# Paired down projection, gate activation and kept sums rearranged in a hybrid encoder layer

## The chip, the core and the metric

The kernel runs on one NeuronCore of one Trainium2 chip. The metric is the device time of one launch in microseconds (us). A core has several engines, each with its own queue of instructions that it works through strictly in order: TensorE (PE in the profile, with its weight loads as PEld), VectorE (DVE), ScalarE (ACT), GpSimd (POOL) and SyncE (SP). DMAs are issued from queues of SP, ACT and POOL and then move data beside the engines. Engines wait for one another on semaphores.

## The reference

One layer of an encoder is applied to two groups of tokens, 256 (prompt) and 512 (sample), all in float32, with a model width of 1024. Three token mixers run first (a diagonal state-space model, differential attention and cross-attention into memory); their outputs are merged and added to x. The change touches only what comes last, the feed-forward part with a hidden width of 2816:

```python
    h2 = rmsnorm(x, ffn_norm_g[li])
    g, up = jnp.split(h2 @ w_gate_up[li], 2, axis=-1)
    x = x + (jax.nn.silu(g) * up) @ w_down[li]
```

## The kernel before, in words

**Products.** All 768 tokens are held as one matrix. Each float32 operand is split into a high and a low part in a TensorE format (`fp32r`), and a product is three matmuls that accumulate in one bank of PSUM: high by high, high by low and low by high (`mm3`, L800 to L802). The high part is written by ScalarE as a copy, the low part by VectorE as a difference (`split_evac`, or L592 and L593 for streamed weights). PSUM is shared out as five banks (`psd`) and three (`psb`).

**Feed-forward in hidden blocks.** The hidden width is cut into 11 blocks of 256, numbered 0 to 10. Block 0 is computed plainly. For blocks 1 to 10, gate and up are each one call of `block`, which works out a product of 2x2 block matrices with Strassen-Winograd's seven products instead of eight: left factors A11, A12, S2, S1, S3, S4, A22 (weights, of which the S are sums made by GpSimd, tiles `ws`), right factors B11, B21, T2, T1, T3, B22, T4 (the normed tokens and their sums, made once). VectorE adds the products into tiles `fs` (L1458), and `fin_gate` and `fin_up` turn finished quarters into the hidden activations `fa`. `fin_gate` makes silu as a Tanh on ScalarE (L1413) and one operation on VectorE (L1414), which leaves twice the silu; the factor 0.5 is put right where the activations are split.

**Down projection.** Block 0 goes through `down_first`. Blocks (1,2), (3,4), (5,6) and (7,8) are taken in pairs by `down_pair`, again with seven products; blocks 9 and 10 go plainly through `down_last`. In a pair the left factors are activations (A11 to A22, sums S1 to S4; function `left` splits them on ScalarE at L1496 and VectorE at L1497, `left_sum` adds on VectorE at L1504) and the right factors are weights of `w_down` (T1 to T4 are sums). Each of the seven products takes three PSUM tiles `dn` of 128x512. `into` adds a product to the residual `x1` on VectorE (L1521). Products 1, 6 and 5 (A11·B11, S2·T2, S1·T1), which several quarters of the result need, are kept instead: `keep` copies each third on ScalarE to a tile `de`, stores it by a DMA of ScalarE's queue to `p_scr`, and for pairs after the first adds it to `p_sum` in DRAM by a DMA of GpSimd's queue (L1558). `down_sums` loads these sums once near the end by SP's DMAs and adds them to `x1` in 21 additions (L1598).

**Weights.** A stream (`W`, class `WStream`) loads weight pieces ahead of their use: raw tiles `wr` (three buffers), split tiles `wh`, `wl` (a ring of four), GpSimd's sums `ws`, and for the down projection two tiles `wt..x` and `wt..z` of 512 KB. `_split_d` makes the right factors in the order of their use. It builds T3 = B22 - B12, T2 = T3 + B11 and T4 = B21 - T2 in place in `wt..x`: a negation on ScalarE (L601), then a DMA on GpSimd's queue that adds a part of `w_down` from DRAM (L600). In the names, wh86 is stream piece 86; with pair 4 (blocks 7 and 8) pieces 85 and 86 are its down weights, 87 is gate 9, 88 up 9 and 89 gate 10.

**What sets the order.** The program is written in one order, and the Tile scheduler places the instructions in each engine's queue by its own simulated times and by when buffers come free. On an engine an instruction that waits holds up everything behind it. Three rings matter here: `lf` holds three left halves (high and low); `ft` has three tiles, which Tanh's results, the `de` of `keep` and the `de` of `down_sums` share; `brr` holds `fs` and the left sums `ls`.

Of the kernel before, what the change touches and what calls it, by code (L numbers as in the profile page):

```python
# [504 lines left out]
class WStream:  # L505
# [90 lines left out]
    def _split_d(self, i, h, kind):  # L596

        r = self.raw.pop(2 * i + h)
        (b11, b12), (b21, b22) = (self.src[j][0] for j in ((i, i + 1) if kind == "d" else (i - 1, i)))
        add = lambda t, b: self.nc.gpsimd.dma_start(t.rearrange("p (k c) -> p k c", k=2), b, accum_op=ALU.add)  # L600
        minus = lambda t, x: self.nc.scalar.activation(t, x, AF.Copy, scale=-1.0)  # L601
        new = lambda k: self.wsums.tile([128, self.HALF], F32, name=f"wt{i}{k}", tag="wt")
        if kind == "d" and h == 0:
            self._right(i, "B11", r)
            self.z = new("z")
            minus(self.z, r)
            add(self.z, b12)
        elif kind == "d":
            self.x = new("x")
            minus(self.x, r)  # L610
            add(self.x, b22)
            self._right(i, "T3", self.x)
        elif h == 0:
            add(self.x, b11)
            self._right(i, "T2", self.x)
            self._right(i, "B21", r)
            self._right(i, "T1", self.z)
        else:
            minus(self.x, self.x)
            add(self.x, b21)  # L620
            self._right(i, "T4", self.x)
            self._right(i, "B22", r)

    def _split(self):
        i, h = divmod(self.n_split, 2)
# [44 lines left out]
def hybrid_block(ctx, tc, A, outs, consts):  # L670
# [737 lines left out]
    act_in = {}  # L1408

    def fin_gate(fb, c, m, cs):  # L1410
        n = cs.stop - cs.start
        t = ft_.tile([128, 512], F32, name=uid("ft"), tag="ft")
        act.activation(t[:, 0:n], c, AF.Tanh, scale=0.5)  # L1413
        v.scalar_tensor_tensor(out=act_in[fb][:, m, cs], in0=t[:, 0:n], scalar=1.0, in1=c, op0=add, op1=mul)  # L1414

    def fin_up(fb, c, m, cs):
        o = act_in[fb][:, m, cs]
        v.tensor_tensor(out=o, in0=o, in1=c, op=mul)
        if fb == 0:
            hh, hl = hid[0]  # L1420
            act.activation(hh[:, m, cs], o, AF.Copy, scale=0.5)
            v.scalar_tensor_tensor(out=hl[:, m, cs], in0=o, scalar=0.5, in1=hh[:, m, cs].bitcast(F32),
                                   op0=mul, op1=sub)

    def new_block(what, fb):
        if what == "gate":
# [66 lines left out]
    def left(key, src):  # L1493

        hi, lo = (lf.tile([128, 2, HT], F32R, name=uid(f"l{key}{w}"), tag="l" + w) for w in "hl")
        act.activation(hi, src, AF.Copy, scale=0.5)  # L1496
        v.scalar_tensor_tensor(out=lo, in0=src, scalar=0.5, in1=hi.bitcast(F32), op0=mul, op1=sub)  # L1497
        L[key] = hi, lo
        return hi, lo

    def left_sum(o, x, y, op):
        if o is None:
            o = stg.tile([128, 2, HT], F32, name=uid("ls"), tag="brr")
        v.tensor_tensor(out=o, in0=x, in1=y, op=op)  # L1504
        return o

    def down_begin(fb):

        a = act_in[fb]
        left("A11", a[:, :, 0:HT])  # L1510
        if fb < NFB - 2:
            left("S3", left_sum(None, a[:, :, 0:HT], a[:, :, HT:TOK], sub))

    def out_block(r, c, t):

# [19 lines left out]
    def down_pair(fb):  # L1535

        a, b = act_in.pop(fb), act_in.pop(fb + 1)
        a11, a21, a12, a22 = a[:, :, 0:HT], a[:, :, HT:TOK], b[:, :, 0:HT], b[:, :, HT:TOK]  # L1540
        R = dict(W.get())
        R.update(W.get())

        def prod(l, r):
            ps = banks()
            rh, rl = R.pop(r)
            rows_times(ps, L.pop(l), (lambda k: rh[:, k], lambda k: rl[:, k]), True, True)
            return ps
# [24 lines left out]
        into(0, 1, prod("S4", "B22"))  # L1573

    def down_last(fb):

        a, b = act_in.pop(fb), act_in.pop(fb + 1)
        w = [W.get(), W.get()]
        for r in range(2):
            h = slice(HT * r, HT * r + HT)  # L1580
            x = [L.pop("A11") if r == 0 else left("A21", a[:, :, h]), left("A2", b[:, :, h])]
            ps = [banks(), banks()]
            for i in range(2):
                for c in range(2):
                    y = [(lambda k, j=j: w[i](k, 512 * c, 512)[j]) for j in range(2)]
                    rows_times(ps[c], x[i], y, i == 0, i == 1)
            for c in range(2):
                into(r, c, ps[c], done=True)

    def down_sums():  # L1590

        for t in range(3):
            e = {}
            for key in "165":
                e[key] = ft_.tile([128, 512], F32, name=uid("de"), tag="ft")
                nc.sync.dma_start(e[key], p_sum[key][:, t])
            b = {(r, c): out_block(r, c, t) for r in range(2) for c in range(2)}
            plus = lambda o, y: v.tensor_tensor(out=o, in0=o, in1=y, op=add)  # L1598
            plus(b[0, 0], e["1"])
            plus(e["6"], e["1"])  # L1600
            plus(b[1, 1], e["6"])
            plus(b[1, 0], b[1, 1])
            plus(b[1, 1], e["5"])
            plus(e["6"], e["5"])
            plus(b[0, 1], e["6"])


    with ExitStack() as c5:
# [210 lines left out]
    W.wsums = c6.enter_context(tc.tile_pool(name="wsum2", bufs=2))  # L1819
    for fb in range(1, NFB):  # L1820
        block("gate", fb)
        if fb == NFB - 2:
            down_sums()
        if fb == 2:
            for t in range(3):
                o = out_block(1, 0, t)

                tc.keep_in_program_order(v.tensor_tensor(out=o, in0=o, in1=out_block(1, 1, t), op=sub))
        if fb % 2 == 0:
            down_begin(fb - 1)  # L1830
        block("up", fb)
        if fb % 2 == 0:
            (down_last if fb == NFB - 1 else down_pair)(fb - 1)
# [45 lines left out]
```

## Time and profile before

| | us |
|---|---|
| median of 3 runs | 1785.59 |
| lowest and highest run | 1784.18, 1787.11 |
| profiled execution, its own time | 1780.15 |
| its span | 1778.4 |
| PE busy | 1748.8 (98% of the span) |
| DVE busy | 1307.2 (74%) |
| ACT busy | 917.3 (52%) |
| POOL busy | 252.0 (14%) |

The four paired down projections begin at 1379.52, 1468.75, 1555.80 and 1644.98 us of the span. Behind the fourth stand gate 9 (from 1678.72), up 9 (1693.31) and gate 10 (1707.87). The profile comes from one execution of the program. Its page lists busy times and the costliest groups of instructions; the trace behind it can be asked for every instruction in a stretch of time, with what it waited for. In a timeline row stand the start, the duration, the engine, the line, the operation, what it writes and reads, and in brackets how long its engine stood idle before it and whose end released it. In a row on windows each engine's busy time is followed by its number of instructions.

### The profile page before, as it was taken

The page shows a single profiled execution, that of the slowest core. Times are in us where ns is not written, and L with a number is a line of the kernel's source. Part 1 is how long each engine was busy: PE and PEld are TensorE (multiplying, and loading weights), DVE is VectorE, ACT ScalarE, POOL GpSimd, SP SyncE. Part 2 cuts the span into 40 slices and gives each one's busy share as a digit, 9 for nine tenths or more (in the row PEclk, how much of TensorE's full clock was granted, in tenths as well). Part 3 has the DMA queues.
Part 4 walks back from the last instruction along what each step waited for, and adds up shares of the span by engine and source line. Part 5 has one row for each costly group of instructions (what it writes and reads, how often), then busy time and mean ns, then how long its engine had stood idle before and what let it go on. Part 6 is the DMA issues. An engine that isn't in the chain of part 4 may idle for free. (4 is left out here: it accounts for less than half of the span.)

```text
span 1778.4 us, 29549 instructions
## 1 busy us (share of the span) xinstructions
PE 1748.8 (98%) x11214; PEld 1611.2 (91%) x11214; DVE 1307.2 (74%) x2409; ACT 917.3 (52%) x1894; POOL 252.0 (14%) x283
## 2 busy tenths in 40 slices
PE   8999999999999999999999999999999999999999
PEld 8999988999999998999978888888889898989787
DVE  7655758799999688878885545452689787879795
ACT  7444544777676457778666333232434545454431
POOL 0000000000000101011110101000113333333330
PEclk9999999999999999999999999999999999999999
DMA  7222656655656477554862635322314447474742
GB/s 255 72 96 95 108 136 159 157 138 138 156 136 162 124 173 194 113 114 90 184 166 75 217 117 171 116 97 70 83 44 112 136 114 174 121 179 115 171 130 83
DMA packets 211565, 235.14 MB, mean 132 GB/s; under 512 B 59232, under 2 KB 169056, under 8 KB 211424
## 3 DMA queue, kind: packets, MB, share of 16 engines
q1 hardware_dynamic: 178000, 149.63, 28.1%
q0 software_dynamic: 27088, 71.05, 19.6%
q10 hardware_dynamic: 6336, 12.59, 1.9%
q8 instruction: 88, 1.44, 0.3%
q14 instruction: 53, 0.43, 0.1%
HBM read 163.94 MB, written 49.09 MB: 120 GB/s over the span
## 5 line engine op out<-in xcount | busy, mean ns | idle before, releaser
L638 ACT ACTIVATE wh<-wr 128x1024 fp32r<-128x1024 f32 x130 | 146.8, 1130 | 74.4 <-PE br L801 27.5
L644 DVE TENSOR_TENSOR wl<-wr,wh 128x1024 fp32r<-128x1024 f32 x84 | 111.0, 1322 | 75.4 <-ACT wh L638 74.8
L800 PE MATMUL gl<-Hhi,wh 128*128 128x256 f32 (+1 forms) x384 | 132.2, 344 | 1.0 <-ACT glt L1110 1.0
L802 PE MATMUL gl<-Hhi,wl 128*128 128x256 f32 (+1 forms) x384 | 128.9, 336 | 0.0
L801 PE MATMUL gl<-Hlo,wh 128*128 128x256 f32 (+1 forms) x384 | 128.8, 336 | 0.0
L642 POOL DMA_DIRECT2D wl<-wr x46 | 40.2, 874 | 516.9 <-ACT wl L641 448.5
L800 PE MATMUL qk<-wh,Hhi 128*128 128x256 f32 x384 | 107.5, 280 | 1.1 <-ACT qksq L1176 1.1
L801 PE MATMUL qk<-wl,Hhi 128*128 128x256 f32 x384 | 107.7, 280 | 0.0
L802 PE MATMUL qk<-wh,Hlo 128*128 128x256 f32 x384 | 107.6, 280 | 0.0
L800 PEld LDWEIGHTS gl<-Hhi,wh 128*128 128x128 f32 x384 | 72.2, 188 | 8.3 <-ACT glt L1110 1.2
L802 PEld LDWEIGHTS gl<-Hhi,wl 128*128 128x128 f32 x384 | 72.0, 188 | 8.0
L801 PEld LDWEIGHTS gl<-Hlo,wh 128*128 128x128 f32 x384 | 72.3, 188 | 7.2
L1276 DVE TENSOR_REDUCE nm<-sc 128x1 f32<-128x512 f32 (+1 forms) x96 | 57.2, 599 | 24.4 <-PE sc L1271 23.1
L800 PEld LDWEIGHTS qk<-wh,Hhi 128*128 128x128 f32 x384 | 72.3, 188 | 2.1 <-ACT qksq L1176 1.3
L802 PEld LDWEIGHTS qk<-wh,Hlo 128*128 128x128 f32 x384 | 72.4, 189 | 0.7
L801 PEld LDWEIGHTS qk<-wl,Hhi 128*128 128x128 f32 x384 | 72.3, 188 | 0.5
L563 ACT ACTIVATE wh_S<-ws 128x512 fp32r<-128x512 f32 x70 | 41.3, 624 | 57.6 <-POOL ws L585 36.1
L564 DVE TENSOR_TENSOR wl_S<-ws,wh_S 128x512 fp32r<-128x512 f32 x70 | 56.2, 823 | 15.6 <-ACT wh_S L563 15.4
L1278 ACT ACTIVATE p<-sc,nm 128x512 f32<-128x512 f32 (+1 forms) x96 | 59.1, 617 | 13.3 <-DVE nm L1276 12.8
L1628 ACT ACTIVATE glr<-glr 128x768 f32<-128x768 f32 x24 | 20.3, 846 | 66.0 <-DMA glr<-gl_scr 64.1
L800 PE MATMUL v<-wh,Hhi 128*128 128x256 f32 x192 | 53.9, 281 | 0.0
L801 PE MATMUL v<-wl,Hhi 128*128 128x256 f32 x192 | 53.8, 280 | 0.0
(582 smaller groups left out, 6209.5 us busy)
## 6 DMA issues: line engine op xcount, KB each, us to landing
wr<-in_w_in_dram SPq DMA_DIRECT2D x48, 512.0 KB, 5.0
wl<-wr POOLq DMA_DIRECT2D x46, 512.0 KB, 5.0
wr<-in_w_gate_up_dram SPq DMA_DIRECT2D x44, 512.0 KB, 4.5
wr<-in_w_branch_dram SPq DMA_DIRECT2D x24, 512.0 KB, 4.4
wr<-in_w_down_dram SPq DMA_DIRECT2D x22, 512.0 KB, 4.4
glr<-gl_scr POOLq DMA_DIRECT2D x24, 384.0 KB, 3.6
wr<-in_w_mem_kv_dram SPq DMA_DIRECT2D x16, 512.0 KB, 3.7
wr<-in_w_in_dram SPq DMA_DIRECT2D x32, 256.0 KB, 4.5
```

The source lines that it names most:

```text
L563: self.nc.scalar.activation(f(hi), src, AF.Copy)
L564: self.nc.vector.tensor_tensor(out=f(lo), in0=src, in1=f(hi).bitcast(F32), op=ALU.subtract)
L638: self.nc.scalar.activation(hi, r, AF.Copy)
L642: self.nc.gpsimd.dma_start(lo, r.bitcast(F32R), accum_op=ALU.add)
L644: self.sub.tensor_tensor(out=lo, in0=r, in1=hi.bitcast(F32), op=ALU.subtract)
L800: pe.matmul(ps, wh, xh, start=start, stop=False)
L801: pe.matmul(ps, wh, xl, start=False, stop=False)
L802: pe.matmul(ps, wl, xh, start=False, stop=stop)
L1276: v.tensor_reduce(out=nm[:, m : m + 1], in_=ps, axis=AX.X, op=ALU.max, negate=True)
L1278: act.activation(pm[:, 0:n], ps, AF.Exp, bias=nm[:, m : m + 1], accum_out=s1s[:, tt : tt + 1] if m == 0 else s2)
L1628: act.activation(g, g, AF.Tanh, scale=0.5)
```

## The change

The program is the same up to the first gate block. From there on:

- **Order of the seven products of a pair.** Before: A11·B11, S3·T3, S2·T2, A12·B21, S1·T1, A22·T4, S4·B22. After: A11·B11, S3·T3, A12·B21, S4·B22, S2·T2, S1·T1, A22·T4. The left halves are made in that order too, and `_split_d` makes the right factors as B21, B22, T2, T1, T4, where they were T2, B21, T1, T4, B22.
- **S4.** It was written over S2's sum late in the pair. It is now made early, in a buffer of its own (tag `do`).
- **Gate activation.** ScalarE's Silu writes `fa` in one call per quarter; Tanh, its temporary tile and VectorE's L1414 are gone. The activations are no longer doubled, so the splits need no 0.5 and are a plain copy and a plain subtraction.
- **Kept sums.** `down_sums` takes a tile number. Tile 0 is added behind gate 9's code, tile 1 behind gate 10's, and tile 2 in `down_last`, where all three stood behind gate 9's code.

```diff
@@ _split_d
         elif h == 0:
             add(self.x, b11)
+            self._right(i, "B21", r)
+        else:
+            self._right(i, "B22", r)
             self._right(i, "T2", self.x)
-            self._right(i, "B21", r)
             self._right(i, "T1", self.z)
-        else:
             minus(self.x, self.x)
             add(self.x, b21)
             self._right(i, "T4", self.x)
-            self._right(i, "B22", r)
@@ fin_gate, fin_up
-        n = cs.stop - cs.start
-        t = ft_.tile([128, 512], F32, name=uid("ft"), tag="ft")
-        act.activation(t[:, 0:n], c, AF.Tanh, scale=0.5)
-        v.scalar_tensor_tensor(out=act_in[fb][:, m, cs], in0=t[:, 0:n], scalar=1.0, in1=c, op0=add, op1=mul)
+        act.activation(act_in[fb][:, m, cs], c, AF.Silu)
...
-            act.activation(hh[:, m, cs], o, AF.Copy, scale=0.5)
-            v.scalar_tensor_tensor(out=hl[:, m, cs], in0=o, scalar=0.5, in1=hh[:, m, cs].bitcast(F32),
-                                   op0=mul, op1=sub)
+            split_evac(hh[:, m, cs], hl[:, m, cs], o)
@@ left, left_sum
-        act.activation(hi, src, AF.Copy, scale=0.5)
-        v.scalar_tensor_tensor(out=lo, in0=src, scalar=0.5, in1=hi.bitcast(F32), op0=mul, op1=sub)
+        split_evac(hi, lo, src)
...
-    def left_sum(o, x, y, op):
-        if o is None:
-            o = stg.tile([128, 2, HT], F32, name=uid("ls"), tag="brr")
+    def left_sum(x, y, op, tag="brr", bufs=2):
+        o = stg.tile([128, 2, HT], F32, name=uid("ls"), tag=tag, bufs=bufs)
@@ down_pair
         keep("1", prod("A11", "B11"))
-        s1 = left_sum(None, a21, a22, add)
-        s2 = left_sum(None, s1, a11, sub)
+        left("A12", a12)
+        s1 = left_sum(a21, a22, add)
+        s2 = left_sum(s1, a11, sub)
+        left("S4", left_sum(a12, s2, sub, "do", 1))
+        into(1, 1, prod("S3", "T3"))
         left("S2", s2)
-        into(1, 1, prod("S3", "T3"))
-        left("A12", a12)
+        into(0, 0, prod("A12", "B21"))
+        left("S1", s1)
+        into(0, 1, prod("S4", "B22"))
+        left("A22", a22)
         keep("6", prod("S2", "T2"))
-        left("S1", s1)
-        into(0, 0, prod("A12", "B21"))
-        left("A22", a22)
         keep("5", prod("S1", "T1"))
-        left("S4", left_sum(s2, a12, s2, sub))
         into(1, 0, prod("A22", "T4"))
-        into(0, 1, prod("S4", "B22"))
@@ down_last, down_sums, the loop over blocks
+            if r == 0:
+                down_sums(2)
...
-    def down_sums():
-
-        for t in range(3):
...
+    def down_sums(t):
...
-        if fb == NFB - 2:
-            down_sums()
+        if fb >= NFB - 2:
+            down_sums(fb - NFB + 2)
```

VectorE's queue at the start of pair 4, before: T2's lower part (`wl86_T2`) stands ahead of the two sums `ls` that make S1 and S2.

```order
L593 TENSOR_TENSOR wl86_T2_18100<-wt85x_17999,wh86_T2_18099 128x1024
L1504 TENSOR_TENSOR ls_1943_18208<-fa_1885_17549,fa_1908_17834 128x768
L1458 TENSOR_TENSOR fs_1928_18009<-fs_1928_18009,up_1935_18125 128x384
L593 TENSOR_TENSOR wl86_B21_18104<-wr86_0_17865,wh86_B21_18103 128x1024
L1418 TENSOR_TENSOR fa_1908_17834<-fa_1908_17834,fs_1928_18009 128x384
L1504 TENSOR_TENSOR ls_1944_18210<-ls_1943_18208,fa_1885_17549 128x768
L593 TENSOR_TENSOR wl86_T1_18108<-wt85z_17994,wh86_T1_18107 128x1024
L1521 TENSOR_TENSOR x1_3_12309<-x1_3_12309,dn_1947_18216 128x512
L1497 SCALAR_TENSOR_TENSOR lS2l_1946_18213<-ls_1944_18210,lS2h_1945_18212 128x768
```

The same place after (line numbers of the changed file; `up_1902` is up 8's last product):

```order
L1453 TENSOR_TENSOR fs_1895_17940<-fs_1895_17940,up_1902_18056 128x384
L1497 TENSOR_TENSOR ls_1912_18143<-fa_1860_17496,fa_1879_17773 128x768
L593 TENSOR_TENSOR wl86_B22_18037<-wr86_1_17928,wh86_B22_18036 128x1024
L1415 TENSOR_TENSOR fa_1879_17773<-fa_1879_17773,fs_1895_17940 128x384
L1497 TENSOR_TENSOR ls_1913_18145<-ls_1912_18143,fa_1860_17496 128x768
L1497 TENSOR_TENSOR ls_1914_18147<-fa_1879_17773,ls_1913_18145 128x768
L593 TENSOR_TENSOR wl86_T2_18041<-wt85x_17930,wh86_T2_18040 128x1024
L1514 TENSOR_TENSOR x1_3_12309<-x1_3_12309,dn_1917_18153 128x512
L794 TENSOR_TENSOR lA12l_1911_18140<-fa_1879_17773,lA12h_1910_18139 128x768
```

T2's lower part has moved behind B22's and behind all three left sums, and S2's lower half, which followed, has given its place to A12's.

GpSimd's queue at pair 4, before: the two adds that make T2 and T4 in `wt85x` stand together, ahead of gate 9's weight sums (`ws87`).

```order
L585 TENSOR_TENSOR ws843_17842<-wr84_1_17695,ws841_17840 128x512
L600 DMA wt85x_17999<-in_w_down_dram 128x2x512 x2
L1558 DMA p_sum1_172<-p_scr_1939_18195 128x512
L578 TENSOR_TENSOR ws870_18146<-wr87_0_18006,wr87_1_18111 128x512
L1558 DMA p_sum1_172<-p_scr_1939_18195 128x512
L579 TENSOR_TENSOR ws871_18147<-ws870_18146,wr87_0_18006 128x512
L583 TENSOR_TENSOR ws872_18148<-wr87_0_18006 128x512
L1558 DMA p_sum1_172<-p_scr_1939_18195 128x512
```

And after:

```order
L585 TENSOR_TENSOR ws843_17781<-wr84_1_17634,ws841_17779 128x512
L600 DMA wt85x_17930<-in_w_down_dram 128x2x512
L578 TENSOR_TENSOR ws870_18077<-wr87_0_17937,wr87_1_18034 128x512
L579 TENSOR_TENSOR ws871_18078<-ws870_18077,wr87_0_17937 128x512
L583 TENSOR_TENSOR ws872_18079<-wr87_0_17937 128x512
L1551 DMA p_sum1_172<-p_scr_1906_18126 128x512 x3
L600 DMA wt85x_17930<-in_w_down_dram 128x2x512
```

The second add, that for T4, has moved behind three weight sums and the three adds of product 1.

VectorE's queue around gate 9's last products, before:

```order
L1458 TENSOR_TENSOR fs_1982_18430<-fs_1982_18430,gate_1987_18463 128x384
L564 TENSOR_TENSOR wl88_S1_18415<-ws880_18402,wh88_S1_18414 128x512
L564 TENSOR_TENSOR wl88_S1_18415<-ws882_18404,wh88_S1_18414 128x512
L1458 TENSOR_TENSOR fs_1983_18431<-fs_1982_18430,gate_1989_18490 128x384
L1458 TENSOR_TENSOR fs_1983_18431<-fs_1983_18431,gate_1988_18477 128x384
L1458 TENSOR_TENSOR fs_1982_18430<-fs_1982_18430,gate_1988_18477 128x384
```

And after, with `gate_1955` for the product that was `gate_1988` (S1·T1):

```order
L1453 TENSOR_TENSOR fs_1950_18362<-fs_1950_18362,gate_1954_18393 128x384
L1592 TENSOR_TENSOR x1_3_12309<-x1_3_12309,de_1961_18471 128x512
L1592 TENSOR_TENSOR de_1960_18469<-de_1960_18469,de_1961_18471 128x512
L1592 TENSOR_TENSOR x1_0_12306<-x1_0_12306,de_1960_18469 128x512
L1592 TENSOR_TENSOR x1_1_12307<-x1_1_12307,de_1981_18757 128x512
L564 TENSOR_TENSOR wl88_S1_18347<-ws880_18334,wh88_S1_18346 128x512
L564 TENSOR_TENSOR wl88_S1_18347<-ws882_18336,wh88_S1_18346 128x512
L1592 TENSOR_TENSOR de_1982_18759<-de_1982_18759,de_1981_18757 128x512
L1453 TENSOR_TENSOR fs_1951_18363<-fs_1950_18362,gate_1956_18420 128x384
L1592 TENSOR_TENSOR x1_4_12310<-x1_4_12310,de_1982_18759 128x512
L1453 TENSOR_TENSOR fs_1951_18363<-fs_1951_18363,gate_1955_18407 128x384
L1453 TENSOR_TENSOR fs_1950_18362<-fs_1950_18362,gate_1955_18407 128x384
```

Additions of the kept sums (L1592, of tile 0 and tile 1), which before stood from up 9 on, now stand in gate 9, between the additions that read gate 9's products out of PSUM.

More of the change, by code (lines that the diff above doesn't have):

```diff
@@ L1511, in down_begin @@
         if fb < NFB - 2:
-            left("S3", left_sum(None, a[:, :, 0:HT], a[:, :, HT:TOK], sub))
+            left("S3", left_sum(a[:, :, 0:HT], a[:, :, HT:TOK], sub))
     def out_block(r, c, t):
@@ L1588, in down_last @@
                 into(r, c, ps[c], done=True)
-    def down_sums():
-        for t in range(3):
[L1593 to L1605, printed above, removed]
+    def down_sums(t):
+        e = {}
+        for key in "165":
+            e[key] = ft_.tile([128, 512], F32, name=uid("de"), tag="ft")
+            nc.sync.dma_start(e[key], p_sum[key][:, t])
+        b = {(r, c): out_block(r, c, t) for r in range(2) for c in range(2)}
+        plus = lambda o, y: v.tensor_tensor(out=o, in0=o, in1=y, op=add)
+        plus(b[0, 0], e["1"])
+        plus(e["6"], e["1"])
+        plus(b[1, 1], e["6"])
+        plus(b[1, 0], b[1, 1])
+        plus(b[1, 1], e["5"])
+        plus(e["6"], e["5"])
+        plus(b[0, 1], e["6"])
     with ExitStack() as c5:
```

## The prediction

> **What bounds the kernel now.** I read the page first, then who TensorE (PE) waits for in the feed-forward part, then that part stage by stage, and last the other engines inside the stages that are long.
>
> ```profile
> span 1778.4 us, 29549 instructions
> PE 1748.8 (98%) x11214; PEld 1611.2 (91%) x11214; DVE 1307.2 (74%) x2409; ACT 917.3 (52%) x1894; POOL 252.0 (14%) x283
> ```
>
> PE is the bound and its matmuls stay the same in number, so the change can only move time in which PE stands still or runs slowly. PE's waits from 1285 us to the end (total, times, longest):
>
> ```profile
> PE dn L800 <- ACT lS2h L1496: 7.3, 3, 3.2
> PE gate L800 <- DVE fs L1458: 2.0, 2, 1.6
> PE dn L800 <- DVE x L1489: 1.0, 1, 1.0
> PE up L800 <- DVE fs L1458: 0.8, 1, 0.8
> ```
>
> The stages by windows: the four paired down projections, then gate 9, up 9 and gate 10. The first number is the length, then PE, PEld, DVE, ACT, POOL, clock, DMA.
>
> ```profile
> 1379.52:1410.48 30.96, 28.91 (x127) 23.57 (x127) 24.97 (x32) 17.86 (x26) 9.93 (x6) 1.00 0.54 155
> 1468.75:1497.53 28.78, 28.78 (x127) 23.57 (x127) 25.41 (x30) 17.35 (x25) 12.03 (x13) 1.00 0.75 175
> 1555.80:1586.71 30.91, 28.91 (x127) 23.57 (x127) 25.48 (x30) 17.34 (x25) 12.34 (x13) 1.00 0.75 175
> 1644.98:1678.72 33.74, 30.51 (x127) 24.70 (x127) 25.40 (x30) 17.62 (x25) 10.83 (x11) 0.95 0.76 172
> 1678.72:1693.31 14.59, 14.59 (x86) 14.58 (x84) 10.92 (x14) 4.79 (x9) 7.86 (x7) 1.00 0.72 174
> 1693.31:1707.87 14.56, 14.56 (x86) 14.56 (x85) 13.78 (x22) 5.71 (x11) 4.90 (x4) 1.00 0.46 145
> 1707.87:1726.66 18.79, 15.83 (x85) 14.29 (x85) 18.64 (x30) 5.74 (x10) 8.10 (x5) 1.00 0.32 105
> ```
>
> The second pair runs without a wait, so 28.78 us is what seven products take (4.11 each). The others lose 2.18, 2.13 and 4.96, together 9.27 us. Gate 10 loses 18.79 - 14.59 = 4.20 us, with DVE busy 18.64 of 18.79. The fourth pair shows the first loss in PE's timeline:
>
> ```profile
> 1652.72 0.39 PE L801 MATMUL dn<-wl_T,lS3h 128*128 128x512 f32 x1
> 1652.95 0.39 PE L802 MATMUL dn<-wh_T,lS3l 128*128 128x512 f32 x1
> 1656.57 0.50 PE L800 MATMUL dn<-wh_T,lS2h 128*128 128x512 f32 x1 [3.23 <-ACT lS2h L1496]
> 1658.60 0.63 PE L801 MATMUL dn<-wl_B,lA12h 128*128 128x512 f32 x1
> 1659.03 0.63 PE L800 MATMUL dn<-wh_B,lA12h 128*128 128x512 f32 x1
> ```
>
> After the 3.23 us wait the matmuls start 0.43 apart instead of 0.23: the clock was halved, which is some 1.6 of the 4.96. The waits of the first and third pair, about 2.2 us each, left the clock at 1.00.
>
> Why S2's left half is late, on ACT and DVE:
>
> ```profile
> 1648.88 1.06 ACT L592 ACTIVATE wh_T<-wt85x 128x1024 fp32r<-128x1024 f32 x1 [9.85 <-DMA wt85x<-in_w_down_dram]
> 1655.68 0.83 ACT L1496 ACTIVATE lS2h<-ls 128x768 fp32r<-128x768 f32 x1
> 1649.97 1.23 DVE L593 TENSOR_TENSOR wl_T<-wt85x,wh_T 128x1024 fp32r<-128x1024 f32 x1 [5.21 <-ACT wh_T L592]
> 1654.17 0.96 DVE L1504 TENSOR_TENSOR ls<-ls,fa 128x768 f32<-128x768 f32 x1
> 1656.47 0.68 DVE L1521 TENSOR_TENSOR x<-x,dn 128x512 f32<-128x512 f32 x1
> ```
>
> T2's parts stand in both queues and wait for the DMA that adds B11 to T3. DVE stood still for 5.21 us; behind it stood the two sums that make S2.
>
> **The change, part by part.** Times below count from the start of a pair's first product.
>
> *Second pair of products.* T2 leaves its early place, and B21 and B22, plain weights already loaded, stand there. S2·T2 becomes the fifth product and has 16.4 us. What is needed next is A12's lower half. DVE's new order gives 0.47 (last gate-up sum) + 0.87 + 1.15 (B22) + 0.5 + 0.87 + 0.87 = 5.0; then T2, whose tile is free when A11·B11 ends at 4.1, so ACT copies it to 5.3 and DVE ends it at 6.5; one evacuation and A12's half end at 8.0. PE wants it behind ten matmuls of the third product, at 10.5. So the 9.27 us go.
>
> *What is late instead: T4.* B21's add that makes T4 needs ACT's negation of T2, now at 9.1. On POOL it used to stand ahead of the sums for the next gate; now three sums and three adds of product 1 stand before it.
>
> ```profile
> 1652.59 1.22 POOL L600 DMA_DIRECT2D wt85x<-in_w_down_dram  x1 [9.12 <-ACT wt85x L601]
> 1663.42 1.29 POOL L578 TENSOR_TENSOR ws<-wr,wr 128x512 f32<-128x512 f32 x1 [7.08 <-issue]
> 1666.64 1.40 POOL L583 TENSOR_TENSOR ws<-wr 128x512 f32<-128x512 f32 x1
> ```
>
> Before, it was issued at 1652.59 - 1644.98 = 7.6. The three sums take 4.6 here with one DMA between them. DMAs by issue and median us to landing, from 1652 to 1700 us; behind them the one B11 add of pair 2 that ran alone, and the least, median and longest of all transfers that touch the kept products:
>
> ```profile
> p_scr<-de ACTq DMA_DIRECT2D x9, 256.0 KB, 6.0
> p_sum<-p_scr POOLq DMA_DIRECT2D x9, 256.0 KB, 6.3
> wt85x<-in_w_down_dram POOLq DMA_DIRECT2D x1, 512.0 KB, 7.8
> de<-p_sum SPq DMA_DIRECT2D x2, 256.0 KB, 3.6
> ...
> wt73x<-in_w_down_dram POOLq DMA_DIRECT2D x1, 512.0 KB, 6.2
> ...
> DMA to landing us min/median/max: 2.0/5.5/12.6
> ```
>
> Product 1's last third is stored at 7.6 and lands at 9.6 at the soonest (2.0), at 13.6 by the median of 6.0; POOL then issues B21's add at 10.4, or 14.2. It lands at 10.4 + 6.2 = 16.6 at best and at 14.2 + 7.8 = 22.0 in traffic. I take the early issue, since little else is in flight there, and 9.4 (between 6.2 and 12.6, for three adds stand ahead in its queue): 19.8. From the landing, ACT's copy 1.06, DVE's 1.23 and two evacuations of S4·B22, 0.6 apart in DVE's queue, make 3.7 with the handovers; PE wants that bank for the last third of S1·T1 at 5 x 4.11 + 2.7 = 23.2. So PE waits when the add lands after 19.5: 0.3 in pairs 2 to 4, 1.0 in all (bounds 0 and 7.5). In pair 1 no kept adds stand on POOL and nothing waits.
> The Trainium skill, "DMA: Bandwidth & Descriptors", section on the anatomy of a DMA on the SWDGE path, fits 2.0 us plus bytes / 436e3, an estimate of 3.2 us for 512 KB. The row above has 6.2 for an add that ran alone, so the measurement decides; by the page T4 would be early and the forecast 1.0 us lower.
>
> *Gate activation by one call.*
>
> ```profile
> L1414 DVE SCALAR_TENSOR_TENSOR fa<-ft,fs 128x384 f32<-128x384 f32 x40 | 28.9, 725 | 7.0 <-ACT ft L1413 5.9
> L1413 ACT ACTIVATE ft<-fs 128x384 f32<-128x384 f32 x40 | 20.8, 521 | 48.4 <-DVE fs L1458 43.4 <-DVE fa L1414 3.8 <-DVE de L1598 1.0
> L1156 ACT ACT_TABLE_LOAD x1 | 1.3, 1283 | 0.0
> ```
>
> DVE loses 40 x 0.725 us and four smaller calls, 31 us in all, of work beside PE. Silu's call has no row; Tanh's of the same shape has 0.521, Copy is near it, and I take 0.521 (twice that would still fit ACT's 52%). One table load of 1.28 us is added at the first gate call, hidden by ACT's idle half; uncovered it costs 1.3 once. Worth on PE: the 1.0 us wait for DVE in the first down projection goes. Halving left out and plain subtraction for the scaled one cost nothing: both forms of 128x768 take 0.95 (below).
>
> ```profile
> L1504 DVE TENSOR_TENSOR ls<-fa,fa 128x768 f32<-128x768 f32 x4 | 3.8, 952 | 0.0
> L1497 DVE SCALAR_TENSOR_TENSOR lS4l<-ls,lS4h 128x768 fp32r<-128x768 f32 x4 | 3.8, 944 | 0.0
> L1598 DVE TENSOR_TENSOR x<-x,de 128x512 f32<-128x512 f32 x12 | 7.8, 678 | 0.0
> ```
>
> S4's own buffer adds no instruction.
>
> *Kept sums.* The 21 adds (0.6 to 0.68 each) left gate 10 short by 4.20 us; that goes. But without Tanh's temporaries in their ring the loads and adds of all three tiles now stand from the start of gate 9 on, with three buffers, ahead of the sums that free gate 9's banks. Products 6 and 5 are now fifth and sixth, so their adds come last. For tile 0 of product 5: issued on POOL behind up 9's first weight sum at 32.1, landed at 38.4 (6.3), loaded by 41.5; three adds of 0.6 free a buffer at 43.3; the next load of product 6 takes about 3, to 46.3; two adds and three gate sums (0.6, 0.47) end at 48.9. PE wants that bank for up 9's second product at 28.8 + 8 x 2.08 = 45.4 (a product is 14.59 / 7). Wait: 3.5 us, and as in pair 4 half a clock behind it, 1.6. New cost 5.1, bounds 0 (adds land 3.5 earlier, the least being 2.0) and 11.7 (12.6 instead of 6.3, the clock halved as well).
>
> **Sum.** -9.27 - 4.20 - 1.0 + 1.0 + 5.1 = -8.4 us. The profiled execution took 1780.15 (span 1778.4), 5.4 under the median 1785.59; the same saving from the median gives 1777.2.
>
> **Rivals.**
> - *Slower: T4 rules.* The add's place behind six instructions on POOL and its 12.6 us longest relative speak for it, the empty DMA queues there against. A wait of 3 us halves the clock as well (1.6). It decides when the add lands after about 22.3: then three pairs lose (2.8 + 1.6) x 3 = 13.2, which with 5.1 exceeds the gain of 14.5 by more than 3.6. At 23.0 it is (3.5 + 1.6) x 3 = 15.3 + 5.1 - 14.5 = +5.9: 1791.5. Chance 0.15. "TensorE: Matmul & The Clock Gate" in the Trainium skill, Part 1, puts the halving at one idle window of about 3.4 us; here 3.23 were enough.
> - *No change: the kept sums hold DVE longer.* The kept adds land 12.6 after issue: 11.7 + 1.0 - 14.5 = -1.8, 1783.8. For it: the median of 6.3 was measured with less in the queue. Against: no load of weights falls there. 0.16.
> - *All hidden:* both new costs are nothing, -14.5: 1771.1. For it: DVE has 31 us less to do. 0.17.
> - *The change doesn't do it:* the wait moves from S2 to A12 unchanged; -14.5 + 9.27 + 6.1 = +0.9, 1786.5. Only 2.5 us of slack speak for it. 0.05.
> - The forecast itself: 0.47.
>
> **Numbers.** 0.2% is 3.6 us, about what can be told from no change. Faster: 0.47 + 0.17 = 0.64; the same 0.16 + 0.05 = 0.21; slower 0.15. The forecast's own range is 1773 to 1782. The range 1771 to 1788 leaves out most of the slower case and half of the hidden one, under 0.2.
>
> **What would show it.** Right: no PE wait for lS2h; the four pairs 28.8 to 30 long with any wait at the sixth or seventh product; gate 10 of 14.6; a wait for DVE at up 9's second product with slow matmuls behind it; no L1414 row; one table load more. Wrong: pairs 2 to 4 over 31 us with ACT idle for the T4 transfer, or a wait in up 9 above 8 us.

## The result

The changed kernel is not faster. Over fourteen runs each its median is 1787.38 us (1784.47 to 1789.64) against 1786.10 us before (1783.48 to 1787.40); the ratio is 1.0011, with a 95% interval of 1.0003 to 1.0018, between 1 and 2 us more. That is within the 0.2% that I called no change, where 8.4 us less had been forecast.

The page of the profile after begins:

```profile
span 1787.7 us, 29494 instructions
PE 1749.0 (98%) x11214; PEld 1611.0 (90%) x11214; DVE 1282.8 (72%) x2365; ACT 921.9 (52%) x1895; POOL 252.0 (14%) x283
```

PE does the same work. DVE has 24.4 us less of it (1307.2 before), and in the total nothing came of that. The two spans (1778.4 and 1787.7) must not be subtracted: the gate of block 0, up to which the programs are the same, began at 1265.15 us in the profile of before and at 1270.33 in this one (1266.84 to 1270.37 in all profiles taken later), so 5.2 us of the 9.3 arose ahead of the change. I compare lengths of stages instead, each from one profile. After, by windows: the four pairs, gate 9, up 9 and gate 10 (length, PE, PEld, DVE, ACT, POOL, granted clock as a share of full speed, DMA share, GB/s):

```profile
1384.59:1413.78 29.19, 28.89 (x128) 23.57 (x127) 26.23 (x31) 17.15 (x25) 9.46 (x7) 1.00 0.50 150
1472.05:1502.19 30.14, 29.18 (x127) 23.49 (x127) 24.24 (x29) 16.42 (x24) 11.67 (x10) 1.00 0.62 140
1560.46:1591.42 30.96, 29.23 (x127) 23.50 (x127) 24.19 (x29) 16.16 (x24) 11.67 (x10) 1.00 0.61 136
1649.69:1680.81 31.12, 29.20 (x128) 23.50 (x128) 23.83 (x28) 15.65 (x23) 10.38 (x10) 1.00 0.57 135
1680.81:1696.68 15.87, 15.04 (x86) 14.51 (x84) 11.71 (x15) 5.87 (x11) 8.48 (x9) 1.00 1.07 265
1696.68:1720.74 24.06, 16.46 (x86) 15.88 (x85) 20.66 (x31) 5.93 (x11) 7.69 (x5) 0.86 0.37 120
1720.74:1736.25 15.51, 14.83 (x85) 14.54 (x85) 15.37 (x26) 6.63 (x12) 6.84 (x5) 1.00 0.22 69
```

And what PE waited for from 1322 us on (total, times, longest):

```profile
PE up L800 <- DVE fs L1453: 7.6, 2, 6.5
PE dn L800 <- DVE x L1514: 3.7, 3, 1.6
...
PE dn L802 <- DVE lA12l L794: 1.2, 4, 0.3
```

S2's waits are gone, as intended. In their place stand three waits in pairs 2 to 4, a small one for A12 in each pair, and one of 6.5 us in up 9. The pairs together take 121.42 us (124.41 before), gate 9 to gate 10 together 55.44 (47.94 before).

**The wait in pair 4.** POOL, ACT and PE:

```profile
1652.09 1.52 POOL L578 TENSOR_TENSOR ws<-wr,wr 128x512 f32<-128x512 f32 x1 [6.88 <-issue]
1653.69 1.50 POOL L579 TENSOR_TENSOR ws<-ws,wr 128x512 f32<-128x512 f32 x1
1655.13 2.02 POOL L583 TENSOR_TENSOR ws<-wr 128x512 f32<-128x512 f32 x1
1657.09 1.72 POOL L1551 DMA_DIRECT2D p_sum<-p_scr  x2
1662.94 0.82 POOL L1551 DMA_DIRECT2D p_sum<-p_scr  x1 [4.13 <-DMA p_scr<-de]
1663.95 1.23 POOL L600 DMA_DIRECT2D wt85x<-in_w_down_dram  x1 [0.18 <-issue]
...
1658.00 0.85 ACT L793 ACTIVATE lS4h<-ls 128x768 fp32r<-128x768 f32 x1 [1.71 <-DVE ls L1497]
1658.01 0.33 ACTq L1549 DMA_DIRECT2D p_scr<-de  x1
...
1671.66 1.06 ACT L592 ACTIVATE wh_T<-wt85x 128x1024 fp32r<-128x1024 f32 x1 [7.37 <-DMA wt85x<-in_w_down_dram]
...
1675.23 0.50 PE L800 MATMUL dn<-wh_T,lS1h 128*128 128x512 f32 x1 [1.62 <-DVE x L1514]
```

Read upwards: PE waits for a bank that DVE frees behind T4's split, ACT gets T4 at 1671.6, POOL issued its add only at 1663.95 (14.3 us after the pair's start), because the last kept add of product 1 ahead of it waited 4.13 us for its store, and that store was issued at 1658.01.

**The wait in up 9.** DVE, SP and PE:

```profile
1695.55 0.54 DVE L1453 TENSOR_TENSOR fs<-fs,gate 128x384 f32<-128x384 f32 x1
1699.32 0.69 DVE L1592 TENSOR_TENSOR x<-x,de 128x512 f32<-128x512 f32 x1 [3.23 <-DMA de<-p_sum]
1704.73 0.54 DVE L1453 TENSOR_TENSOR fs<-fs,gate 128x384 f32<-128x384 f32 x1
...
1689.82 0.99 SPq L544 DMA_DIRECT2D wr<-in_w_gate_up_dram  x2
1692.55 9.13 SPq L1590 DMA_DIRECT2D de<-p_sum  x4
...
1698.58 0.34 PE L802 MATMUL up<-fhi,wl_A 128*128 128x384 f32 x1
1705.42 0.66 PE L800 MATMUL up<-fhi,wh_A 128*128 128x384 f32 x1 [6.50 <-DVE fs L1453]
1705.88 0.52 PE L801 MATMUL up<-flo,wh_A 128*128 128x384 f32 x1
1706.20 0.52 PE L802 MATMUL up<-fhi,wl_A 128*128 128x384 f32 x1
```

Between two additions that read gate 9's products (1695.55 and 1704.73) DVE works through additions of the kept sums that the scheduler has moved forward (hoisted, as I call it below), and whose loads SP issued at 1692.55 and later. Up 9's second product needs the bank that the later one frees, and behind the wait the matmuls start 0.32 instead of 0.17 apart.

### The profile page after: what moved, and what is told of

The parts are those of the page before. It is cut to its first block, busy times and chain, and to the rows that moved or that the text cites. A ratio compares the mean times of both kernels' runs of the same rounds, so it can differ in the third digit from the quotient of the medians.

```text
span 1787.7 us, 29494 instructions
## 1 busy us (share of the span) xinstructions
PE 1749.0 (98%) x11214; PEld 1611.0 (90%) x11214; DVE 1282.8 (72%) x2365; ACT 921.9 (52%) x1895; POOL 252.0 (14%) x283
## 3 DMA queue, kind: packets, MB, share of 16 engines
q0 software_dynamic: 27088, 71.05, 19.5%
## 4 chain that ended last, share of the span: by engine, by line
PE 79%; DMA 7%; DVE 6%; issue 5%; ACT 2%; POOL 1%; SPq 0%; ACTq 0%; POOLq 0%; DVEq 0%
PE gl L800 3%; PE gl L801 3%; PE gl L802 3%; PE br L801 3%; PE br L800 3%; PE br L802 3%; PE gate L800 3%; PE gate L801 3%; PE gate L802 3%; PE up L800 2%; PE up L802 2%; PE up L801 2%; PE qk L801 2%; PE qk L802 2%; PE qk L800 2%
## 5 line engine op out<-in xcount | busy, mean ns | idle before, releaser
L644 DVE TENSOR_TENSOR wl<-wr,wh 128x1024 fp32r<-128x1024 f32 x84 | 111.0, 1322 | 78.0 <-ACT wh L638 77.4
```

Source lines behind the costliest of these rows:

```text
L644: self.sub.tensor_tensor(out=lo, in0=r, in1=hi.bitcast(F32), op=ALU.subtract)
```

## The experiments

The lengths of the stages in every profile, from the starts of the first matmuls of each (us; the ratio is to the kernel before, run on the same chip, with its 95% interval):

| kernel | four pairs | gate 9 | up 9 | gate 10 | up 10 and last | ratio |
|---|---|---|---|---|---|---|
| before | 124.41 | 14.59 | 14.56 | 18.79 | 51.72 | 1 |
| changed | 121.42 | 15.87 | 24.06 | 15.51 | 51.49 | 1.0011 (1.0003 to 1.0018) |
| e1_t4_first | 116.80 | 15.60 | 21.69 | 17.13 | 51.49 | 0.9988 (0.9979 to 0.9997) |
| e2_sums_held | 121.73 | 14.59 | 14.56 | 14.56 | 52.66 | 0.9956 (0.9938 to 0.9973) |
| e7_pool_clear | 114.40 | 15.25 | 24.83 | 16.31 | 51.50 | 0.9995 (0.9985 to 1.0005) |
| e3_both | 114.41 | 14.59 | 14.56 | 14.56 | 52.66 | 0.9915 (0.9902 to 0.9929) |
| e4_order_only | 122.68 | 14.59 | 14.56 | 17.68 | 51.72 | 0.9971 (0.9958 to 0.9983) |
| e5_silu_only | 116.83 | 23.78 | 19.31 | 14.56 | 51.49 | 1.0004 (0.9995 to 1.0013) |
| e6_sums_only | 124.84 | 14.59 | 14.56 | 16.44 | 51.59 | 0.9974 (0.9960 to 0.9987) |
| e10_tanh_back | 122.73 | 14.59 | 14.56 | 14.56 | 51.49 | 0.9958 (0.9944 to 0.9973) |
| e8_sums_earlier | 114.4 | 14.59 | 14.56 | 15.20 | 56.13 | 0.9937 (0.9922 to 0.9952) |
| e9_kept_first | 114.4 | 16.63 | 21.49 | 14.56 | 51.50 | 0.9971 (0.9960 to 0.9981) |

My theory after the first look: two losses eat the gain, T4's add by its place on POOL and the hoisted sums on VectorE. The rivals: the traffic of the DMAs, and that the sums are late because T4 is.

### T4's add ahead of the kept adds of product 1

What is traced under `issue_after` is queued behind the instruction named, on its engine.

```diff
-            add(self.x, b21)
+            self.t4 = add(self.x, b21)
...
-                    gp.dma_start(p_sum[key][:, t], d[:, t], accum_op=add)
+                    with tc.issue_after(W.t4.ins):
+                        gp.dma_start(p_sum[key][:, t], d[:, t], accum_op=add)
```

> The changed kernel, with one thing altered: on POOL the three adds of product 1 to the kept sums stand behind the add of B21 that makes T4, instead of ahead of it. Theory (T4 is late by its place on POOL): the add was issued 14.3 us after the start of pair 4 because it stood behind the third kept add, which waited for a store that landed at 12.8; now it waits for ACT's negation of T2 alone and is issued at about 10.7, as in pair 1, where it was 10.8. It lands at 17 to 18 and PE no longer waits for it in pairs 2 to 4, which become 29.2 us like pair 1 (30.15, 30.97, 31.11 now), 4.7 us less. ACT's copies of product 6, which stood behind T4's split, come 3 to 4 us earlier, and the wait at up 9's second product (6.84) shrinks by about as much: some 8 us less than the changed kernel in all, about 1779. Rival (the traffic of the DMAs sets the landing, wherever the add stands): the add takes as much longer as it is issued earlier, the pairs stay near 31 and the time stays at 1787.

Measured: 1781.78 us, ratio 0.9988. The pairs are 29.20, 29.19, 29.21 and 29.20, and no wait for T4 is left. POOL's add and the window of pair 4:

```profile
1656.88 1.22 POOL L600 DMA_DIRECT2D wt85x<-in_w_down_dram  x1 [3.34 <-ACT wt85x L601]
```

```profile
1646.08:1675.28 29.20, 28.90 (x127) 23.58 (x127) 26.46 (x30) 17.26 (x25) 13.22 (x12) 1.00 0.69 172
```

It goes 10.8 us after the pair's start, 3.5 earlier, and landed 6.2 us later (7.6 in the changed kernel): the place in the queue made T4 late, far more than the traffic. The second half of the expectation failed. Gate 9 to gate 10 came down only from 55.44 to 54.42, so most of what delays the kept sums is not T4.

### POOL's queue cleared

The weight sums of the next gate are queued behind T4's add as well; the edit above stays.

```diff
-        gt = self.nc.gpsimd.tensor_tensor
+        def gt(**kw):
+            if self.t4 is None:
+                return self.nc.gpsimd.tensor_tensor(**kw)
+            with self.issue_after(self.t4.ins):
+                return self.nc.gpsimd.tensor_tensor(**kw)
```

> The changed kernel, with POOL's queue cleared ahead of T4's add: the add of B21 stands ahead of the kept adds of product 1 and of the weight sums of the next gate as well. Besides the place in the queue this takes away the sums that ran on POOL 2.4 to 7.4 us after the start of each pair, while VectorE's three operations beside them took 1.64, 1.94 and 1.93 us instead of 0.56, 0.95 and 0.95. Theory (the two slowed each other): those three come back to 0.56 and 0.95, A12's lower half is ready 3 us earlier and its 0.3 us wait goes in all four pairs, T2's negation and so T4's add is issued at about 8 instead of 14.3 and lands before 16; all four pairs are 28.8, 6.3 us less than the changed kernel, and up 9's wait shrinks by 4 to 6: about 1776. Rival (VectorE was slow for another reason, its operands or its partner ACT): the three operations stay at 1.6 to 1.9, the pairs come only to 29.2 as with the place in the queue alone.

Measured: 1783.20 us, ratio 0.9995. DVE at the start of pair 4, in the changed kernel and then here:

```profile
1652.38 1.64 DVE L1415 TENSOR_TENSOR fa<-fa,fs 128x384 f32<-128x384 f32 x1
1654.06 1.94 DVE L1497 TENSOR_TENSOR ls<-ls,fa 128x768 f32<-128x768 f32 x1
1656.03 1.93 DVE L1497 TENSOR_TENSOR ls<-fa,ls 128x768 f32<-128x768 f32 x1
```

```profile
1644.84 0.55 DVE L1421 TENSOR_TENSOR fa<-fa,fs 128x384 f32<-128x384 f32 x1
1645.43 0.96 DVE L1503 TENSOR_TENSOR ls<-ls,fa 128x768 f32<-128x768 f32 x1
1646.42 0.96 DVE L1503 TENSOR_TENSOR ls<-fa,ls 128x768 f32<-128x768 f32 x1
```

The same three operations took 5.51 us beside POOL's sums and 2.47 without them, so the rival (operands or ACT) falls. With POOL moved, A12's wait went too and all four pairs are 28.60, the length without any wait. But up 9 did not gain. Windows of pair 4 and up 9, and POOL in gate 9:

```profile
1642.15:1670.75 28.60, 28.60 (x127) 23.66 (x127) 27.66 (x32) 17.38 (x25) 11.53 (x10) 1.00 0.73 167
...
1686.00:1710.83 24.83, 17.27 (x86) 16.69 (x85) 19.86 (x30) 5.93 (x11) 6.85 (x5) 0.79 0.43 141
```

```profile
1674.62 1.30 POOL L573 TENSOR_TENSOR ws<-wr,wr 128x512 f32<-128x512 f32 x1 [6.13 <-DMA wr<-in_w_gate_up_dram]
1675.85 1.65 POOL L1558 DMA_DIRECT2D p_sum<-p_scr  x2
```

The kept adds of products 6 and 5 now stand behind a weight sum that waits for a load. So this run alone can't tell whether an early T4 helps the sums; the run before it, without that wait, had already left 54.42 of the 55.44.

### The kept adds ahead of up 9's weight sums

```diff
+            if fb == 7 and key == "5":
+                W.t4 = o
```

(`o` is the last kept add of product 5, behind which the next weight sums are queued; SP's queue, too, then has the third load ahead of the next weights.)

> The changed kernel with POOL's queue cleared ahead of T4's add (e7_pool_clear), and in pair 4 the kept adds of products 6 and 5 ahead of up 9's weight sums on POOL; the additions stay hoisted. There T4 was early and up 9 took 24.8 us all the same: the last add of product 6 could have gone at 1669.6, when its store had landed, and went at 1675.9, behind a weight sum that waited for a load. Theory (the kept adds wait for weights on POOL, and the hoisted additions for the kept adds): those adds go 5 us earlier, the loads for tile 0 are in by then, and up 9 comes to 18 to 20 us, with gate 9 still 15 to 16: 4 to 6 us less than with POOL's queue cleared alone. Rival (SP's queue and the ring of three hold the loads, wherever the adds stand): up 9 stays at 23 to 25.

Measured: 1779.31 us, ratio 0.9971 against 0.9995 with POOL cleared alone, 4.3 us. Gate 9 to gate 10 take 52.68 instead of 56.39. Gate 9 took 16.63 (15 to 16 expected) and up 9 21.49, not 18 to 20; its longest wait, 3.5 us, now stands at S1·T1. So the kept adds' place on POOL is a part of the loss in the kernel with POOL cleared, whose own queue had put them behind that weight sum. Against the changed kernel's 55.44 only 2.8 us come back, and 9.0 of the loss stay while the additions are hoisted.

### The kept sums held at their place

```diff
-            nc.sync.dma_start(e[key], p_sum[key][:, t])
+            tc.keep_in_program_order(nc.sync.dma_start(e[key], p_sum[key][:, t]))
...
-        plus = lambda o, y: v.tensor_tensor(out=o, in0=o, in1=y, op=add)
+        plus = lambda o, y: tc.keep_in_program_order(v.tensor_tensor(out=o, in0=o, in1=y, op=add))
```

> The changed kernel, with one thing altered: the loads and the additions of the kept sums are held at their place in the program on SP and on VectorE: tile 0 behind gate 9, tile 1 behind gate 10, tile 2 in the last down projection. Theory (the hoisted additions block VectorE while their loads are under way): gate 9 comes back to 14.6 us (15.87 now), up 9 to 14.6 (24.06), gate 10 to 14.6 (15.51); the pairs stay as they are, T4 late. That is 11.7 us less than the changed kernel, about 1775.7. Rival (the kept sums are late because T4 held ACT's copies back, and whoever needs them waits): the wait only moves on to up 9's later products and gate 10, and less than half of the 11.7 comes back, 1782 or more.

Measured: 1776.38 us, ratio 0.9956. Gate 9, up 9 and gate 10 are 14.59, 14.56 and 14.56 with T4 as late as ever (pairs of 29.2 to 31.0). The hoist, of loads and additions together, is the cause, and the rival, by which the wait would move on, falls. The last stretch took 1.2 us more, with tile 2's additions in it.

### Both

> The changed kernel with both: POOL's queue cleared ahead of T4's add, and the kept sums held at their place in the program. Theory: the two losses are apart from each other; pairs of 28.8 (6.3 us less than the changed kernel), gate 9, up 9 and gate 10 of 14.6 each (11.7 less): 18 us less, about 1769.4, which is 0.9% under the kernel before. Rival (the additions must stand somewhere and VectorE has no room for them in gate 10 and the last projection either): the last stretch grows by 2 to 4 us, 1772 to 1774.

Measured: 1769.04 us, ratio 0.9915 (0.9902 to 0.9929): 15 us less than the kernel before, and the best version found. Its windows: pair 4, gate 9, up 9, gate 10, last projection.

```profile
1642.18:1670.78 28.60, 28.60 (x128) 23.65 (x127) 27.68 (x32) 17.39 (x25) 11.55 (x10) 1.00 0.73 167
1670.78:1685.37 14.59, 14.59 (x86) 14.59 (x85) 9.23 (x15) 6.35 (x12) 10.27 (x10) 1.00 0.88 209
1685.37:1699.93 14.56, 14.56 (x86) 14.56 (x86) 10.86 (x18) 3.73 (x7) 4.92 (x3) 1.00 0.44 132
1699.93:1714.49 14.56, 14.56 (x86) 14.56 (x86) 14.11 (x23) 6.15 (x12) 6.38 (x5) 1.00 0.23 73
1729.04:1767.14 38.10, 32.85 (x145) 26.84 (x144) 19.51 (x31) 3.49 (x4) 0.00 (x0) 0.98 0.25 92
```

In the first four PE is busy for their whole length. By stages the two losses add up: the pairs are as long as with POOL cleared alone, and gate 9 to gate 10 as long as with the sums held alone. The last stretch grew by 1.2 us, not by the rival's 2 to 4. By the ratios the repairs bring 0.0016 and 0.0055 alone and 0.0096 together; the difference of 0.0025 is about as large as the four intervals leave open, so it is not shown that one helps the other.

### The held places moved earlier

Tile 1 behind up 9 and tile 2 behind gate 10, to free the last stretch.

```diff
-            if r == 0:
-                down_sums(2)
...
-            down_sums(fb - NFB + 2)
+            down_sums(0 if fb == NFB - 2 else 2)
...
         block("up", fb)
+        if fb == NFB - 2:
+            down_sums(1)
```

> The kernel with POOL's queue cleared and the kept sums held (e3_both), with the held places moved: tile 0 behind gate 9, tile 1 behind up 9, tile 2 behind gate 10. Theory: the last stretch was 38.1 us with tile 2's additions in it and 36.9 where they stood earlier; this brings it back to 36.9 without a wait elsewhere, since VectorE has room in up 9 and up 10 once Silu is in: 1.2 us less, about 1768. Rival (VectorE has no room for seven additions in up 9 beside its own work): up 9 or gate 10 grow by 1 to 4 us and it is 1770 or more.

Measured: 1772.42 us, ratio 0.9937, 4 us more than the ratio of 0.9915 without this move. The last projection is 36.94 as expected, but gate 10 grew by 0.6 and up 10 from 14.56 to 19.19: a wait of 2.9 us for DVE at its second product, and slow matmuls behind it (the clock over the stage was 0.91). In gate 10 DVE stood 0.49 and 1.17 us for loads of `de` ahead of what it owed PE. It is the wait of up 9 again, one block later. The rival had the time right, and the place only in part: most of the loss is in up 10.

### Each part alone

The order of the products alone (right factors and S4's buffer with it):

> The kernel before with the order alone: the product order of the pairs, the order of the right factors and S4's own buffer; Tanh and all kept sums behind gate 9 as before. Theory: the pairs become those of the changed kernel, 29.2 for the first and 30 to 31 for the others with T4 late, 121.4 us together instead of 124.4; without Silu the three tiles for loads stay shared with Tanh, the additions stay where they were, and gate 10 keeps its loss of 4.2. About 3 us less than before, ratio 0.998. Rival (the kept sums of products 6 and 5, now the last but one, come too late whatever VectorE's order): up 9 or gate 10 grow by another 3 to 7 us and the time is at or above that of before.

Measured: 1778.68 us, ratio 0.9971, 5 us less; the stages of its profile, from the slowest of its eight runs, show 2.8. The pairs are 29.9, 30.4, 31.2 and 31.3: no wait for S2, T4 late as in the changed kernel. Gate 10 keeps most of its loss. The rival falls.

Silu alone:

> The kernel before with Silu alone: one ScalarE call per quarter, plain splits; product order and the place of the kept sums in the program as before. Theory (the freed ring lets the additions move forward, whatever their place in the program): the additions stand in gate 9 and up 9; since products 6 and 5 are third and fifth here, their kept sums land about 4 us earlier against gate 9 than in the changed kernel, so up 9 loses 0 to 5 us where the changed kernel loses 9.5; gate 10's 4.2 go, S2's waits (9.3) stay. 1 to 5 us less than before. Rival (31 us less on VectorE also bring S2 earlier): the pairs come to 122 or less.

Measured: 1783.91 us, ratio 1.0004. Windows of pair 4, gate 9 and up 9, and PE's longest wait:

```profile
1644.47:1674.09 29.62, 28.89 (x127) 23.57 (x127) 24.21 (x28) 17.33 (x25) 12.28 (x13) 1.00 0.72 171
1674.09:1697.87 23.78, 16.34 (x86) 16.02 (x84) 13.82 (x21) 5.00 (x9) 5.61 (x5) 0.86 0.72 189
1697.87:1717.18 19.31, 15.35 (x85) 14.48 (x85) 18.94 (x29) 5.76 (x11) 6.85 (x5) 1.00 0.32 96
```

```profile
PE gate L800 <- DVE x L1515: 7.4, 1, 7.4
```

I was wrong on both sides. The rival was right on the pairs: with less on VectorE they came to 116.8 without any change of order, 7.6 us less. PE's waits for S2 came to 1.5 us in all, from 7.3; in pair 4 POOL issued the add that makes T2 4.8 us ahead of the pair's start, where it had been 2.7. And gate 9 and up 9 lost 13.9 us, not 0 to 5. Eight of the 21 additions stood ahead of the first that reads gate 9's products, the others among those of gate 9 and up 9, and the first of them stood between the fourth pair's last evacuations, whose banks gate 9 needs.

The kept sums tile by tile alone:

> The kernel before with the kept sums tile by tile alone: Tanh and the product order as before. Theory: with Tanh in the ring the additions follow the program's places, tile 0 in up 9, tiles 1 and 2 in up 10; gate 10 comes back from 18.8 to 14.6 and the last stretch grows by 0 to 2: 2 to 4 us less than before, ratio 0.998. Rival (the additions only move the loss on): up 10 and the last projection, 51.7 together, grow by 3 to 5 and nothing is gained.

Measured: 1780.13 us, ratio 0.9974. Gate 10 came to 16.4, not to 14.6, and the last stretch did not grow. The pairs show how S2's wait varies: 31.5, 28.7, 34.9 and 29.8 in the order of before, which had 31.0, 28.8, 30.9 and 33.7.

Everything but Silu:

```diff
-        act.activation(act_in[fb][:, m, cs], c, AF.Silu)
+        n = cs.stop - cs.start
+        t = ft_.tile([128, 512], F32, name=uid("ft"), tag="ft")
+        act.activation(t[:, 0:n], c, AF.Tanh, scale=0.5)
+        v.scalar_tensor_tensor(out=act_in[fb][:, m, cs], in0=t[:, 0:n], scalar=1.0, in1=c, op0=add, op1=mul)
...
```

(The rest of the edit brings the 0.5 in the splits back.)

> The changed kernel with Tanh back (order and kept sums as changed, the gate activation and the splits as before). Theory (it is the ring freed by Silu that moves the additions ahead of what VectorE owes PE): the additions stand in up 9 and up 10; gate 9 and gate 10 are 14.6 and up 9 at most 17; the pairs stay at 121.4 with T4 late. 6 to 8 us less than the changed kernel though it has 31 us more work on VectorE, about 1780. Rival (the kept sums are simply too late for an addition near up 9): up 9 or gate 10 still lose 5 to 10, 1785 or more.

Measured: 1775.57 us, ratio 0.9958, 9.5 us less than the changed kernel by the ratios. Gate 9, up 9 and gate 10:

```profile
1682.34:1696.93 14.59, 14.59 (x86) 14.59 (x85) 13.86 (x19) 7.23 (x14) 10.22 (x9) 1.00 1.05 239
1696.93:1711.49 14.56, 14.56 (x86) 14.56 (x86) 13.91 (x22) 4.37 (x9) 6.75 (x4) 1.00 0.43 139
1711.49:1726.05 14.56, 14.56 (x86) 14.56 (x86) 14.09 (x24) 6.59 (x13) 6.71 (x5) 1.00 0.24 73
```

DVE is busier in gate 9 than in the changed kernel (13.86 against 11.71) and PE never waits. The part that takes 23.4 us off VectorE (1306.2 busy here, 1282.8 in the changed kernel) is the one that makes the change a loss. How it does so can be read from what SP's loads of the kept sums waited for, here and then in the changed kernel:

```profile
SPq L1596 <- DVE fa L1414: 1.8, 2, 1.0
```

```profile
SPq L1590 <- DMA p_scr<-de: 6.7, 2, 5.3
```

(Total, times and longest wait, in us.) With Tanh, loads wait for the operation that reads Tanh's tile, and the first goes at 1698.86, in up 9. Without it none waits for a gate activation; two wait for the stores that `keep` makes from the same ring, and the first load goes at 1683.05, early in gate 9. So Tanh's tile had kept the ring of three busy and the additions late. Whether the smaller work on VectorE alone would also have moved them is not shown: no run has Silu with the ring held, or Tanh with a ring of its own.

## Why the prediction was wrong

By stage lengths of the two profiles, the forecast's sum beside what came (us):

| step | forecast | measured | from |
|---|---|---|---|
| S2's waits go | -9.27 | -9.27 | no wait for lS2h left |
| T4 is late, and A12 | +1.0 | +6.30 | pairs 121.42 - 4 x 28.78 |
| gate 10's shortage goes | -4.20 | -4.23 | before 47.94 for three stages, 43.71 in e10 |
| kept sums moved forward | +5.1 | +11.73 | changed 55.44 against 43.71 |
| first down projection | -1.0 | -0.11 | 114.37 to 114.26 from block 0's gate to pair 1 |
| up 10 and last | 0 | -0.23 | 51.72 to 51.49 |
| sum | -8.4 | +4.2 | the fourteen runs give 1 to 2 |

The measured column comes from one profile each, and S2's loss in particular varies from run to run (e6).

**Right.** S2's waits went for the reason given: the order alone (e4) removes them. The mechanism of both new costs was right too, engine and product: PE waits for the bank of S1·T1's last third, and for up 9's second product. Pair 1, with no kept adds on POOL, has no wait for T4, as forecast. The point from which T4 costs was put at a landing 19.5 us after the pair's start; landings at 20.89 and 21.87 in pairs 2 and 4 left PE waiting 0.7 and 1.6, so it lay at 20.2.

**Wrong, first: the term for T4.** The step that failed is the choice between the two issues that I had worked out, 10.4 and 14.2 us: "I take the early issue, since little else is in flight there". It went at 14.3 in pair 4 and landed at 21.9 instead of 19.8. The store ahead of it was issued at 8.3, not 7.6, and took 4.45 us to land, not the least of 2.0. Of the 6.30, T4 is 4.62 (121.42 to 116.80 in e1). The other 1.68 is A12, which the forecast had put at nothing: POOL's three weight sums, whose new place I had used for the queue alone, also slowed DVE's three operations by 3 us. So DVE's new order, put at 5.0 (its terms add to 4.73), took 8.3, A12's half came at 10.9 instead of 8.0 against a need at 10.5 (a wait of 0.3 us in each pair), and ACT's copy of S4, behind which the store stood, waited for DVE. That is a small part of the last rival, by which the wait would move to A12. e7 shows the cause: with POOL moved, all of that is gone, and the pairs of 28.60 show that the second pair's 28.78, read as free of waits, still held 0.18.

**Wrong, second: the term for the kept sums.** 5.1 was forecast, for up 9 alone, and 11.73 came: 1.28 in gate 9, 9.50 in up 9 and 0.95 in gate 10. The step that failed is the chain for product 5 of tile 0. From the start of pair 4 it was issued on POOL at 34.6 (32.1 forecast), landed at 42.8 (38.4), was loaded at 49.6 (41.5) and freed PE at 55.7 (48.9). The largest part is the load: I had given it 3 us after the landing, but on SP it stood beside two weight loads and took 6.7; the issue was 2.5 later and the landing took 1.9 more. That the upper bound was 11.7 is luck: it stood for a landing 12.6 us after the issue, which took 8.2, and its own terms (5.1, and 6.3 for the later landing) add to 11.4. That the delay comes from T4, which I thought next, is refuted for its greater part by e1; that holding loads and additions back removes all of it is shown by e2.

**The Silu term.** Its calls took 0.52 us each (0.521 taken) and the table load 1.28 on ACT. What I had put at 1.0 us on PE came to about 0.1: the wait for DVE in the first down projection shrank from 1.0 to 0.2, but the first product of block 1's gate waited 0.7 for DVE instead of 0.2; why is open. From block 0's gate to pair 1 all kernels with Tanh take 114.36 to 114.43 and all with Silu 114.26 to 114.31. Of the 31 us off DVE 24.4 were left, for the most part because eight of the sums `ls` took 1.94 us beside POOL instead of 0.95. Alone, Silu brings another 7.6 us in the pairs (e5), which the new order had already taken.

**The rivals.** The one whose price came is "the kept sums hold DVE longer", though not by its condition, as said, and with it a milder form of "T4 rules". I had given both low chances as if only one could come, and each was priced with the other at its mild value. Both stand on POOL's queue, and yet they hang together little: e1 takes T4's loss away and leaves 54.42 us in gate 9 to gate 10, and e2 takes the kept sums' loss away with T4 late.

## What to carry to other kernels

An instruction that leaves an engine also leaves the ring whose buffers it held, and the scheduler may then move other work forward into a place where it waits; look at what the freed buffers release, not only at the time saved. Work on an in-order engine that waits for a DMA belongs behind what that engine owes the bottleneck. A pin to its place in the program was enough here (e2), and a pin to a place too early cost again (e8). When a sum has two uncertain waits, price the case in which both come at the long end, too.

## What the runs showed of the hardware

- POOL's sums slowed DVE. DVE's three operations on two SBUF tiles each took 1.64, 1.94 and 1.93 us beside them and 0.55, 0.96 and 0.96 without. POOL's three took 1.52, 1.50 and 2.02, against means of 1.50, 1.52 and 1.62 in the kernel before, so only the last was clearly longer. The Trainium skill, "SBUF — State Buffer", section "Who interferes with whom", says that a DVE instruction with two SBUF inputs contends with a GpSimd instruction that reads SBUF, through one read interface that they share. The trace agrees. This rule spoke against the change and I had not weighed it.
- PE's waits of 1.6 us (changed kernel, pair 4) and 2.6 us (e6, pair 1) left the granted clock at 1.00. Behind 2.9 us in up 10 of e8 it was 0.91 over the stage, and behind the 6.5 us in up 9 0.86; there the matmuls started 0.32 us apart instead of 0.17.
- A kept sum's load of 256 KB took 2.6 us late in up 9, when little else moved, and 6.7 us beside two weight loads.
